# The output projection in native float32 instead of three float32r passes

## Chip, core and metric

The kernel runs on one core of one Trainium2 chip. The metric is the device time of one execution in microseconds (us).

## What is computed

One block of a streaming encoder on x of shape (1, 2048, 1024) in float32: normed rows go through one input projection (1024 to 2560); of its five parts of 512 columns three feed stick-breaking attention with 8 heads and two a gated position mixing. Both results are normed, joined, and projected back:

```python
a_out = rmsnorm(a_out, out_norm_g[layer, :SB_WIDTH])
b_out = rmsnorm(b_out, out_norm_g[layer, SB_WIDTH:])
mix = jnp.concatenate([a_out, b_out], axis=-1)
x = x + jnp.einsum('bse,ed->bsd', mix, w_out[layer])          # the output projection
h = rmsnorm(x, norm_mlp_g[layer])
act = jnp.square(jax.nn.relu(jnp.einsum('bsd,df->bsf', h, w_up[layer])))
x = x + jnp.einsum('bsf,fd->bsd', act, w_down[layer])
return rmsnorm(x, norm_final_g)
```

The output projection multiplies 2048 x 1024 by 1024 x 1024.

## The kernel before

**Tiling.** The 2048 rows go in four chunks of 512 (TC), each of four row blocks of 128. Matmul operands are kept as two float32r halves, hi and lo, made by `split` (lines 78 to 85): ScalarE writes hi (line 81, or line 84 where a column of factors is multiplied in), VectorE writes lo = source - hi (line 82, or 85). `mm3` (lines 87 to 90) then issues three matmuls for a product: hi x hi, hi x lo, lo x hi, all into one PSUM tile.

**Order.** Each engine runs its instructions in the order in which the program issues them. `together` advances one generator (`main`) step by step and, after each step, the attention generator (`side`) by a ratio, 0.8 in the output projection of chunks 0 and 1 (R_O). So projection, attention and MLP are interleaved on TensorE in an order that is fixed in the program. Chunks 0 and 1 run their last part beside attention; after attention has ended, chunks 2 and 3 run together: operands of chunk 3, its projection, operands of chunk 2, its projection, with the end of chunk 1's MLP and the turning of rows between them.

**Output projection.** `out_operands` (lines 421 to 457) loads the gated rows (`b_d`, tile `o_st`), squares them for the norm, transposes them on TensorE (line 438) and splits them from PSUM into `bm` (line 440); it loads the attention rows (`a_d`), which already lie the other way around, and splits them into `am` (line 455). Both live in tiles named `hT` (for chunk 3 `hTx`, on the other side of SBUF). POOL adds up the squares of the attention rows in `a_sq` (line 454). `out_weights` loads four slices of 128 x 512 of w_out and splits them with the factor `outg` (line 460, through `weight` and lines 84 and 85); SyncE's queue issues the loads. `out` (lines 463 to 489) runs four groups, two column halves times two operands; a group has four row blocks, and each row block takes four products (e = 0 to 3) of a 128 x 128 piece of `hT` with a 128 x 512 piece of `w`, twelve matmuls, into one of three PSUM tiles `mm` (one of five for chunk 3). VectorE adds the result to `y` with the row factor (line 478). Line 484 sums the squares over partitions by native float32 matmuls of one column.

Native float32 matmuls stand in two more places: line 239 (position mixing, 128 columns) and line 153 (128 columns). Lines 334, 438 and 501 are transposes.

`turn` (from line 491) norms the new rows and transposes them for the MLP; `up` and `down` use `mm3` too and aren't touched.

Of the kernel before, what the change touches and what calls it, by code (L numbers as in the profile page):

```python
# [16 lines left out]
P = 128  # L17
# [17 lines left out]
def block_kernel(ctx: ExitStack, tc: tile.TileContext, x, x_t, gmix, w_in, ln_g, ln_b, sgw, sgb,  # L35
# [4 lines left out]

    # ---- constants
    ident = const.tile([P, P], F32, name="ident")
# [19 lines left out]

    # ---- what one phase leaves for another
    q_d = dram.tile([NH, 2, HD, T], F32, name="q_d")
# [5 lines left out]
    def rsqrt_mean(pool, ssq, n, count, tag):  # L70
        """(ssq / count + EPS) ** -0.5 over [P, n]"""
        m = pool.tile([P, NTB], F32, name=f"{tag}_m", bufs=2)
        nc.vector.tensor_scalar(m[:, :n], ssq, 1.0 / count, EPS, ALU.mult, ALU.add)
        r = pool.tile([P, NTB], F32, name=f"{tag}_r", bufs=2)
        nc.gpsimd.tensor_tensor(r[:, :n], m[:, :n], mhalf[:, :n], ALU.pow)
        return r

    def split(hi, lo, src, scale=None):
        """hi + lo = src (times scale), hi and lo of 12 bits each"""
        if scale is None:  # L80
            nc.scalar.activation(hi, src, AF.Copy)  # L81
            nc.vector.tensor_tensor(lo, src, hi.bitcast(F32), ALU.subtract)  # L82
        else:
            nc.scalar.activation(hi, src, AF.Copy, scale=scale)
            nc.vector.scalar_tensor_tensor(lo, src, scale, hi.bitcast(F32), ALU.mult, ALU.subtract)
# [5 lines left out]

    # ---------------------------------------------------------------- projection
    class Rows:
        """where the normalized rows of one chunk live during the projection"""

# [12 lines left out]
    def proj(cs, places, sp, gated_first):  # L108
        """q, k, v and the gated rows of the chunks cs; the rows' 1 / rms joins after the products"""
        rs, r_rows = [], []  # L110
# [38 lines left out]
        def spread(pl, r4):  # L149
            """the chunk's r along the free axis, on all partitions"""  # L150
            ps = pl.ps()
            for tb in range(NTB):
                nc.tensor.matmul(ps[:, tb * P:(tb + 1) * P], r4[tb].broadcast_to([P, P]), ident,
                                 start=True, stop=True)
            rr = sp.tile([P, TC], F32, name="r_row", bufs=2)
            nc.scalar.activation(rr, ps, AF.Copy)
            r_rows.append(rr)
# [37 lines left out]
        def evac_v(pl, t0, i, ps):  # L195
            st = sp.tile([P, NH, 2, HD], F32R, name="qkv_st", bufs=2)
            split(st[:, :, 0, :], st[:, :, 1, :], ps.rearrange("p (h d) -> p h d", d=HD), rs[i])
            # the last ones don't hold up the loads behind them
            queue = nc.scalar if cs[-1] == NC - 1 else nc.sync
            queue.dma_start(v_d[t0 // TC, :, :, t0 % TC // P].rearrange("h p x d -> p h x d"), st.bitcast(F32))  # L200

        def gelu(dst, ps, r):
            """x * sigmoid(2 sqrt(2/pi) (x + a x^3)), the tanh form, of x = r ps"""
            t = sp.tile([P, 512], F32, name="gelu_t", bufs=3)
            nc.scalar.activation(dst, ps, AF.Copy, scale=r)
            nc.scalar.activation(t, dst, AF.Square)
            nc.vector.tensor_scalar(t, t, GELU_A, 1.0, ALU.mult, ALU.add)
            nc.vector.tensor_tensor(t, t, dst, ALU.mult)
            nc.scalar.activation(t, t, AF.Sigmoid, scale=GELU_B)
            nc.vector.tensor_tensor(dst, dst, t, ALU.mult)  # L210
# [61 lines left out]

    # ---------------------------------------------------------------- attention
    NKK = 3
# [5 lines left out]
    def attention(cs):  # L280
        """a step: weights of one block of queries, transposes of an earlier one, product with v of one before"""
        units = [(c, h, seg) for c in cs for h in range(NH) for seg in range(c, -1, -1)]
        state = {}

        def weigh(u, tb):
# [20 lines left out]
            ql = qt[:, tb * P:(tb + 1) * P]  # L306
            # fewer than 256 columns would take longer
            Z = max(L, 2 * P)
# [66 lines left out]

    # ---------------------------------------------------------------- output projection, MLP
    FG, RL_BUFS, ST_BUFS, W_BUFS = 2, 2, 4, 9
    NG = DFF // (P * FG)

    class Place:  # L380
        """where the rows of one chunk live"""

# [5 lines left out]

        def hT(self):
            return self.pool.tile([P, 2, 4, TC], F32R, name=f"hT{self.tag}", bufs=2)  # L390

# [6 lines left out]
    class Block:  # L398
        """the last part of the chunks cs, weights loaded once for all of them"""

# [4 lines left out]
        def normed_rows(self, src, dst, gain, tag):  # L405
            """dst = RMS norm of the rows of src [P, D], with the gain"""
            mp = self.mp
            junk = mp.tile([P, D], BF16, name="rl", bufs=RL_BUFS)
            ssq = mp.tile([P, 1], F32, name=f"{tag}_ssq", bufs=2)
            nc.scalar.activation(junk, src, AF.Square, accum_out=ssq)  # L410
            r = rsqrt_mean(mp, ssq, 1, D, tag)
            nc.vector.scalar_tensor_tensor(dst, src, r[:, 0:1], gain, ALU.mult, ALU.mult)
# [8 lines left out]
        def out_operands(self, i, weights_too=False):  # L421
            mp, c, pl = self.mp, self.cs[i], self.places[i]
            # b part
            bm, rbs = pl.hT(), []
            for tb in range(NTB):
# [13 lines left out]
                ts_ = slice(tb * P, (tb + 1) * P)  # L439
                split(bm[:, 0, :, ts_], bm[:, 1, :, ts_], ps)  # L440
            yield
            ws = self.out_weights(0, 1) if weights_too else None
            # a part
            am = pl.hT()
            total = mp.tile([P, TC], F32, name="a_sq", bufs=1)
            for e in range(4):
                st = mp.tile([P, TC], F32, name="o_st", bufs=4)
                nc.sync.dma_start(st, a_d[e * P:(e + 1) * P, c * TC:(c + 1) * TC])
                if e == 0:
                    nc.scalar.activation(total, st, AF.Square)  # L450
                else:
                    sq = mp.tile([P, TC], F32, name="rl", bufs=RL_BUFS)
                    nc.scalar.activation(sq, st, AF.Square)
                    nc.gpsimd.tensor_tensor(total, total, sq, ALU.add)
                split(am[:, 0, e, :], am[:, 1, e, :], st)
            self.mix[i] = bm, rbs, ws, am, total
            yield

        def out_weights(self, half, part):
            return [self.weight([512], w_out[k * P:(k + 1) * P, half * 512:(half + 1) * 512], outg_t[:, k:k + 1])  # L460
                    for k in range(part * 4, part * 4 + 4)]

        def out(self, i):
            """the rows of x plus the output projection"""
            c, pl = self.cs[i], self.places[i]
# [5 lines left out]
            def group(half, part, m, ws, rr):  # L471
                hs = slice(half * 512, (half + 1) * 512)
                for tb in range(NTB):
                    ts_ = slice(tb * P, (tb + 1) * P)
                    ps = pl.ps()
                    for e in range(4):
                        mm3(ps, m[:, 0, e, ts_], m[:, 1, e, ts_], ws[e][:, 0, :], ws[e][:, 1, :], e == 0, e == 3)
                    nc.vector.scalar_tensor_tensor(ys[tb][:, hs], ps, rr[tb], ys[tb][:, hs], ALU.mult, ALU.add)
                    yield
# [11 lines left out]
        def turn(self, i):  # L491
            """normed rows, split, the other way around"""
            pl = self.places[i]
# [13 lines left out]
        def up(self, fg):  # L507
# [3 lines left out]
            wus = []  # L511
            # the first group goes by half chunks, whose rows are ready earlier
            parts = 2 if fg == 0 else 1
# [29 lines left out]
        def down(self, fg, acts, finish=False):  # L543
            """finish: both halves of a row block at once, so that its rows are done early"""
            def half_weights(half):
# [42 lines left out]
        def middle(self):  # L588
            """all but the last product; returns that one"""
            acts = yield from self.up(0)  # L590
# [8 lines left out]
    def together(main, side=None, ratio=0.0):  # L599
        """side advances by ratio steps per step of main, up to the end of main, whose return value is returned,  # L600
        or of side (then OPEN is)"""
        due = 0.0
# [13 lines left out]
    ps_mm = ctx.enter_context(tc.tile_pool(name="ps_mm", bufs=3, space=PSUM))  # L616
    # what is free first at the end of the projection lies lowest, where the next pool's first tiles come
    ln_g_t = sp.tile([P, 512], F32, name="ln_g_t")
# [106 lines left out]
```

## Time and profile before

| | us |
|---|---|
| median of the two runs | 2592.94 |
| lowest and highest | 2591.4, 2594.48 |
| profiled execution, span from first to last instruction | 2591.2 |
| TensorE busy in it | 2521.4 |
| VectorE busy | 1795.8 |
| ScalarE busy | 1223.2 |
| POOL busy | 164.4 |

For the profiled execution the profile states its span alone; the two runs lie 0.2 and 3.3 us above it. Durations below come from that execution. PE is TensorE, PEld its weight loads, DVE VectorE, ACT ScalarE, SP SyncE, and L90 is line 90 of the kernel. Matmuls are pipelined and their ends are modelled, so that what one costs in a row of them is read from the distance of their starts, and not from its duration.

### The profile page before, as it was taken

What the parts mean: (1) busy time and instruction counts of PE and PEld (TensorE: products, weight loads), DVE (VectorE), ACT (ScalarE), POOL (GpSimd) and SP (SyncE); (2) the same over time, 40 slices, a digit from 0 to 9 for tenths busy, and PEclk for the clock granted to TensorE, in tenths of its full rate; (3) what the DMA queues carried; (4) which work ended last, traced back from release to release, by engine and by line L of the source; (5) the groups of instructions that cost most, each with busy time, mean ns of one, the idle gap of its engine ahead of it and who ended that gap; (6) DMA issues with size and microseconds to landing.
All of it is one profiled execution on the core that took longest, in us unless ns stands there. A gap on an engine that the chain in (4) does not pass through costs nothing.

```text
span 2591.2 us, 33154 instructions
## 1 busy us (share of the span) xinstructions
PE 2521.4 (97%) x11904; PEld 2047.3 (79%) x11904; DVE 1795.8 (69%) x2722; ACT 1223.2 (47%) x2306; POOL 164.4 (6%) x175
## 2 busy tenths in 40 slices
PE   7999998999999999999999999999999999999998
PEld 5788776777878888777788888877888888888886
DVE  6634688778888888899888888875833434344445
ACT  6314456455556555565655555663533232222222
POOL 3200022010000000011000000011100000000000
PEclk9999999999999999999999999999999999999999
DMA  6246756556443444346343334343311111111111
GB/s 211 97 127 207 217 158 193 155 175 192 130 123 118 122 123 122 122 123 196 98 121 116 117 117 122 108 145 98 131 54 47 46 49 49 49 49 45 45 45 66
DMA packets 160229, 299.99 MB, mean 116 GB/s; under 512 B 16576, under 2 KB 32960, under 8 KB 160064
## 3 DMA queue, kind: packets, MB, share of 16 engines
q1 hardware_dynamic: 155760, 295.77, 37.1%
q10 hardware_dynamic: 4304, 2.10, 0.3%
q8 instruction: 94, 1.54, 0.3%
q14 instruction: 71, 0.58, 0.1%
HBM read 255.86 MB, written 41.94 MB: 115 GB/s over the span
## 4 chain that ended last, share of the span: by engine, by line
PE 70%; DVE 20%; DMA 3%; issue 3%; ACT 3%; POOL 1%; SPq 0%; DVEq 0%; POOLq 0%; ACTq 0%
PE mm L89 20%; PE mm L90 20%; PE mm L88 20%; DVE pr L323 4%; DVE y L557 3%; PE tr L334 3%; DVE aT L82 2%; DVE b L324 2%; PE av L352 2%; PE av L353 2%; PE z L309 1%; PE z L310 1%; DVE pr L320 1%; DMA st<-in_w_in 1%; DVE w L82 1%
## 5 line engine op out<-in xcount | busy, mean ns | idle before, releaser
L81 ACT ACTIVATE w<-w_st 128x512 fp32r<-128x512 f32 x384 | 242.7, 634 | 457.1 <-PE mm L90 442.9
L82 DVE TENSOR_TENSOR w<-w_st,w 128x512 fp32r<-128x512 f32 x384 | 259.9, 685 | 163.8 <-ACT w L81 163.7
L90 PE MATMUL mm<-hT,w 128*128 128x512 f32 (+1 forms) x816 | 309.7, 379 | 0.0
L89 PE MATMUL mm<-hT,w 128*128 128x512 f32 (+1 forms) x816 | 308.7, 378 | 0.0
L88 PE MATMUL mm<-hT,w 128*128 128x512 f32 (+1 forms) x816 | 308.6, 378 | 0.1
L88 PE MATMUL mm<-w,act 128*128 128x512 f32 x768 | 300.8, 392 | 2.1 <-DVE y L557 1.4
L90 PE MATMUL mm<-w,act 128*128 128x512 f32 x768 | 301.6, 393 | 0.0
L89 PE MATMUL mm<-w,act 128*128 128x512 f32 x768 | 300.6, 391 | 0.0
L557 DVE TENSOR_TENSOR y<-mm,y 128x512 f32<-128x512 f32 x384 | 257.7, 684 | 49.9 <-PE mm L90 49.3
L323 DVE TENSOR_TENSOR_SCAN pr<-kk,pr,zeros 128x513 f32<-128x513 f32 x192 | 245.4, 1279 | 33.8 <-ACT kk L315 33.7
L315 ACT ACTIVATE kk<-z 128x512 f32<-128x512 f32 (+2 forms) x320 | 168.7, 527 | 176.4 <-PE z L310 122.3
L535 ACT ACTIVATE rl<-mm 128x512 f32<-128x512 f32 x128 | 76.5, 597 | 327.1 <-PE mm L90 326.9
L82 DVE TENSOR_TENSOR aT<-tr,aT 128x512 fp32r<-128x512 f32 (+1 forms) x320 | 190.7, 596 | 6.9 <-ACT aT L81 6.9
L334 PE MATMUL tr<-ident,b 128*128 128x128 f32 x1088 | 180.2, 275 | 6.1 <-DVE b L324 2.6
L81 ACT ACTIVATE aT<-tr 128x512 fp32r<-128x512 f32 (+1 forms) x320 | 172.7, 540 | 21.0 <-PE tr L334 20.4
L88 PEld LDWEIGHTS mm<-hT,w 128*128 128x128 f32 x816 | 154.0, 189 | 30.3 <-DVE y L557 0.5
L82 DVE TENSOR_TENSOR act<-rl,act 128x512 fp32r<-128x512 f32 x96 | 65.8, 686 | 161.0 <-ACT act L81 159.9
L90 PEld LDWEIGHTS mm<-hT,w 128*128 128x128 f32 x816 | 153.5, 188 | 29.4
L89 PEld LDWEIGHTS mm<-hT,w 128*128 128x128 f32 x816 | 153.5, 188 | 29.2
L88 PEld LDWEIGHTS mm<-w,act 128*128 128x128 f32 x768 | 144.6, 188 | 36.2 <-DVE y L557 3.7
L317 ACT ACTIVATE b<-z 128x512 f32<-128x512 f32 (+2 forms) x320 | 169.9, 531 | 0.0
L90 PEld LDWEIGHTS mm<-w,act 128*128 128x128 f32 x768 | 144.1, 188 | 31.3
(185 smaller groups left out, 5272.0 us busy)
## 6 DMA issues: line engine op xcount, KB each, us to landing
w_st<-in_w_up SPq DMA_DIRECT2D x192, 256.0 KB, 2.8
w_st<-in_w_down SPq DMA_DIRECT2D x192, 256.0 KB, 2.8
kt<-k_d SPq DMA_DIRECT2D x160, 256.0 KB, 4.7
st<-in_w_in SPq DMA_DIRECT2D x60, 512.0 KB, 5.2
vt<-v_d SPq DMA_DIRECT2D x80, 256.0 KB, 3.0
w_st<-in_w_out SPq DMA_DIRECT2D x64, 256.0 KB, 3.4
st<-in_x_t SPq DMA_DIRECT2D x16, 512.0 KB, 4.8
st<-in_x SPq DMA_DIRECT2D x16, 512.0 KB, 4.8
```

What stands on the lines that cost most here:

```text
L81: nc.scalar.activation(hi, src, AF.Copy)
L82: nc.vector.tensor_tensor(lo, src, hi.bitcast(F32), ALU.subtract)
L88: nc.tensor.matmul(ps, lh, rh, start=first, stop=False)
L89: nc.tensor.matmul(ps, lh, rl, start=False, stop=False)
L90: nc.tensor.matmul(ps, ll, rh, start=False, stop=last)
L315: nc.scalar.activation(kk[:, :L], z[:, :L], AF.Sigmoid, scale=-QK_SCALE)
L317: nc.scalar.activation(b[:, :L], z[:, :L], AF.Sigmoid, scale=QK_SCALE)
L323: nc.vector.tensor_tensor_scan(pr[:, ::-1], kk[:, ::-1], zeros, carry[tb], ALU.mult, ALU.add)
L324: nc.vector.tensor_tensor(b, b, pr[:, 1:TC + 1], ALU.mult)
L334: nc.tensor.transpose(tr[:, tb * P:(tb + 1) * P], bs[tb][:, j * P:(j + 1) * P], ident)
L535: nc.scalar.activation(rl, ps, AF.Relu)
L557: nc.vector.tensor_tensor(y[:, hs], ps, y[:, hs], ALU.add)
```

## The change

The operands of the output projection are no longer split. `hT` tiles for `bm` and `am` become float32, and VectorE copies the transposed rows and the attention rows into their first half; ScalarE writes the scaled weights as float32 into the first half of `w`, and the low half isn't made. Each product is one matmul on float32 operands where it was three on float32r operands. Sizes and numbers of the tiles stay, and so do all DMAs; the MLP, the attention and the input projection are as before. (The diff also drops comments, which are left out here.)

```diff
-        def hT(self):
-            return self.pool.tile([P, 2, 4, TC], F32R, name=f"hT{self.tag}", bufs=2)
+        def hT(self, dtype=F32R):
+            return self.pool.tile([P, 2, 4, TC], dtype, name=f"hT{self.tag}", bufs=2)
...
-            bm, rbs = pl.hT(), []
+            bm, rbs = pl.hT(F32), []
...
-                split(bm[:, 0, :, ts_], bm[:, 1, :, ts_], ps)
+                nc.vector.tensor_copy(bm[:, 0, :, ts_], ps)
...
-            am = pl.hT()
+            am = pl.hT(F32)
...
-                split(am[:, 0, e, :], am[:, 1, e, :], st)
+                nc.vector.tensor_copy(am[:, 0, e, :], st)
...
         def out_weights(self, half, part):
-            return [self.weight([512], w_out[k * P:(k + 1) * P, half * 512:(half + 1) * 512], outg_t[:, k:k + 1])
-                    for k in range(part * 4, part * 4 + 4)]
+            ws = []
+            for k in range(part * 4, part * 4 + 4):
+                st = self.mp.tile([P, 512], F32, name="w_st", bufs=ST_BUFS)
+                nc.sync.dma_start(st, w_out[k * P:(k + 1) * P, half * 512:(half + 1) * 512])
+                w = self.mp.tile([P, 2, 512], F32, name="w", bufs=W_BUFS)
+                nc.scalar.activation(w[:, 0], st, AF.Copy, scale=outg_t[:, k:k + 1])
+                ws.append(w)
+            return ws
...
                     for e in range(4):
-                        mm3(ps, m[:, 0, e, ts_], m[:, 1, e, ts_], ws[e][:, 0, :], ws[e][:, 1, :], e == 0, e == 3)
+                        nc.tensor.matmul(ps, m[:, 0, e, ts_], ws[e][:, 0, :], start=e == 0, stop=e == 3)
```

## Rows read from the trace of the kernel before

**Rows 1.** The page, parts 1 and 2: busy time; granted clock in tenths.

```profile
PE 2521.4 (97%) x11904; PEld 2047.3 (79%) x11904; DVE 1795.8 (69%) x2722; ACT 1223.2 (47%) x2306; POOL 164.4 (6%) x175
...
PEclk9999999999999999999999999999999999999999
```

**Rows 2.** The page, part 4: the chain that ended last, by line.

```profile
PE mm L89 20%; PE mm L90 20%; PE mm L88 20%; DVE pr L323 4%; DVE y L557 3%; PE tr L334 3%; DVE aT L82 2%; DVE b L324 2%; PE av L352 2%; PE av L353 2%; PE z L309 1%; PE z L310 1%; DVE pr L320 1%; DMA st<-in_w_in 1%; DVE w L82 1%
```

**Rows 3.** Stretches: from:to, length, busy PE, PEld, DVE, ACT, POOL; clock, DMA.

```profile
584.00:638.00 54.00, 52.39 (x258) 42.37 (x256) 46.21 (x73) 28.62 (x54) 3.56 (x6) 1.00 0.67 213
1178.00:1246.00 68.00, 64.80 (x316) 52.26 (x314) 63.38 (x96) 37.22 (x73) 4.95 (x7) 1.00 0.55 168
1755.70:1801.40 45.70, 45.70 (x201) 36.89 (x200) 22.56 (x33) 11.00 (x17) 1.46 (x1) 1.00 0.24 81
1817.00:1868.30 51.30, 49.94 (x239) 40.76 (x238) 40.53 (x68) 24.90 (x46) 7.67 (x10) 1.00 0.46 154
```

**Rows 4.** Groups by line and form, PE: count | busy us, mean ns | idle before.

```profile
L89 PE MATMUL mm<-w,hT 128*128 128x512 f32 x192 | 75.9, 396 | 0.0
...
L89 PE MATMUL mm<-w,hTx 128*128 128x512 f32 x64 | 25.5, 399 | 0.0
```

**Rows 5.** Timeline of PE in chunk 2's projection: start us, us, instruction.

```profile
1842.33 0.39 PE L88 MATMUL mm<-w,hT 128*128 128x512 f32 x1
...
1853.21 0.39 PE L88 MATMUL mm<-w,hT 128*128 128x512 f32 x1
```

**Rows 6.** Timeline of PE in chunk 3's projection.

```profile
1758.51 0.39 PE L88 MATMUL mm<-w,hTx 128*128 128x512 f32 x1
...
1764.11 0.39 PE L88 MATMUL mm<-w,hTx 128*128 128x512 f32 x1
```

**Rows 7.** Lines 239 and 484, native float32: durations ns min/median/max, first and last start.

```profile
L239 PE MATMUL mm<-vn,sgw_t x96: 270/275/275, 81.1 to 475.9; 128*128 128x128 f32 x96
...
L484 PE MATMUL mm<-ones,a_sq x32: 164/250/250, 591.4 to 1834.1; 128*128 128x1 f32 x32
```

**Rows 8.** The chain in order of time, two native pieces: start us, us, what.

```profile
81.23 1.78 PE mm L239 x16
...
591.55 0.79 PE mm L484 x8
```

**Rows 9.** Float32r of 256 columns: its group, then PE's timeline in chunk 2's first up.

```profile
L89 PE MATMUL mm<-hT,w 128*128 128x256 f32 x96 | 27.1, 283 | 0.0
...
1878.08 0.28 PE L88 MATMUL mm<-hT,w 128*128 128x256 f32 x1
...
1879.88 0.28 PE L88 MATMUL mm<-hT,w 128*128 128x256 f32 x1
```

**Rows 10.** Groups by line and form, DVE and ACT.

```profile
L85 DVE SCALAR_TENSOR_TENSOR w<-w_st,outg_t,w 128x512 fp32r<-128x512 f32 x64 | 47.3, 762 | 8.6 <-ACT w L84 8.3
...
L207 DVE TENSOR_SCALAR gelu_t<-gelu_t 128x512 f32<-128x512 f32 x32 | 19.9, 623 | 18.4 <-ACT gelu_t L206 18.1
...
L82 DVE TENSOR_TENSOR hT<-o_st,hT 128x512 fp32r<-128x512 f32 x12 | 12.7, 1075 | 1.9 <-ACT hT L81 1.8
...
L84 ACT ACTIVATE w<-w_st,outg_t 128x512 fp32r<-128x512 f32 x64 | 44.6, 723 | 51.5 <-PE mm L90 32.4 <-DMA w_st<-in_w_out 18.8
```

**Rows 11.** PE's waits (us, times, longest) in 564:587, 1145:1187 and 1801:1822.

```profile
PE mm L88 <- ACT w L84: 1.0, 1, 1.0
PE mm L88 <- DVE hT L82: 1.0, 1, 1.0
...
PE av L353 <- DVE aT L82: 2.3, 5, 0.9
...
PE mm L88 <- DVE y L557: 0.8, 1, 0.8
PE mm L438 <- DVE hT L82: 0.8, 1, 0.8
```

**Rows 12.** A stretch after chunk 0's operands, columns as in group 3.

```profile
578.10:581.50 3.40, 3.40 (x8) 2.50 (x9) 3.40 (x4) 3.40 (x7) 1.72 (x2) 0.54 0.92 281
```

## Prediction

> **What bounds the kernel now.** I read the page's parts on busy time and clock first. TensorE is busy for 2521.4 of 2591.2 us and its granted clock stands at the full 2.4 GHz level in all forty slices to within a tenth [rows 1]. The chain that ended last, by line, runs 20% each through L88, L89 and L90, the three lines of mm3 [rows 2]. So a change in the number or price of matmuls goes nearly straight into the time, unless the stretch in which it lies has idle TensorE time. That I read from the busy time by stretch, with one stretch for each of the four runs of the output projection (chunk 0, chunk 1, chunk 3, chunk 2, in this order of time): TensorE is busy for 52.4 of 54, 64.8 of 68, 45.7 of 45.7 and 49.9 of 51.3 us [rows 3]. VectorE is second (93% busy in chunk 1's stretch), but TensorE is the bound in all four. The whole projection is therefore a sum of matmul prices, corrected by a few us of idle time.
>
> **What the change removes and adds on TensorE.** There are 4 chunks, 4 groups each, 4 row blocks and 4 slices: 256 products of 128x128 by 128x512. The groups by line and form show them as 192 records on each of three lines for the chunks in hT and 64 on each for chunk 3 in hTx [rows 4]: 768 matmuls go.
>
> The duration of one (396 and 399 ns) includes the way through the array and is no price; the price is the distance of starts. In hT, 48 records lie between the starts at 1842.33 and 1853.21: 10.88 / 48 = 227 ns each, 680 ns a product [rows 5]. In hTx, 24 records lie between 1758.51 and 1764.11: 233 ns each, 700 ns a product [rows 6].
>
> What a native float32 product of 512 columns costs no row shows. The nearest rows are native products of other sizes. L239 multiplies in float32 already, with 128 columns: 64 products in the code, but 128 records (96 in vn here, 32 in vnx), and L484 (one column) has 32 records for 16 products [rows 7]. So one native instruction is two records, each with its own weight load, where a float32r one is one record. The changed projection is then 512 records where it was 768.
>
> Now the price of a record. Sixteen native records of 128 columns advance the chain by 1.78 us, 111 ns each; eight of one column advance it by 0.79 us, 99 ns each [rows 8]. Nearly the same for 128 times the columns: at this size the weight load sets the distance, and 111 ns is only an upper bound for streaming 128 columns. Taken up to 512 columns it bounds a record at 4 x 111.3 = 445, say 448 ns, a product at 896 ns. From below, a record can't be cheaper than a float32r one of the same size, since both stream 512 four-byte columns: 227 ns, a product at 453 ns.
>
> Between them I go by durations. Float32r records of 256 columns last 283 ns and start 120 ns apart (15 between 1878.08 and 1879.88) [rows 9]; with 512 columns they start 227 ns apart. So a column streams in (227 - 120) / 256 = 0.417 ns, one cycle at 2.4 GHz, and 13 ns are fixed. The shortest native record of one column lasts 164 ns and the shortest of 128 columns 270 ns [rows 7]: 106 ns for 127 columns, 0.83 ns a column, two cycles. A native record of 128 columns lasts about as long as a float32r record of 256. I take two cycles: 427 ns for 512 columns. The fixed part can't be more than 111.3 - 106.7 = 4.6 ns, or 128 columns would be further apart than they are. One record is then 431 ns and one product 863 ns; in hTx, where a float32r record costs 6.6 ns more, 876 ns.
>
> A rule of the Trainium skill speaks against the change in the same direction. FP8 and Floating Point Precision, section TensorE Precision Notes, says that true FP32 takes four passes through the array, where the split takes three. If each pass cost what a float32r matmul costs here, fixed part included, the sum would be larger than mine; it has its own place among the rivals.
>
> The sum on TensorE: (863 - 680) x 192 = +35.1 us, (876 - 700) x 64 = +11.3 us, together **+46.4 us**. With no fixed part (854 ns everywhere): 33.4 + 9.9 = +43 us. With 448 ns a record, and the surcharge in hTx: 41.5 + 13.4 = +55 us.
>
> **What it takes from the other engines.** VectorE loses the 64 low halves of the output weights at L85, 47.3 us, and ScalarE the high halves of the operands. In out_operands 32 subtractions at L82 become 32 copies; those from o_st are long today (1075 ns mean) [rows 10]. The trace has no float32 copy on VectorE; a single-source operation of 128x512 in SBUF takes 623 ns at L207, so I put a copy there, with the 1075 ns of today's operation as the upper bound and nothing as the lower, none of it on the path. ScalarE keeps the 64 scaled copies at L84, 723 ns each. No DMA comes or goes: the 64 loads of w_out stay on SP's queue in the same place.
>
> All this lies beside TensorE, so it pays only where TensorE waits today. Around the four operand stages these waits are: chunk 0, 1.0 us for the weights from ScalarE and 1.0 us for hT from VectorE; chunk 1, five waits of 2.3 us for aT, while VectorE is behind with operands and weights; chunk 2, 0.8 us for hT and 0.8 us for y [rows 11]. Together 5.9 us. Part stays: the copy of hT still stands in VectorE's queue behind attention's scans. I take 4 us. The most that could go is these and all idle time of the four stretches, 5.9 + (1.6 + 3.2 + 0 + 1.4 from the four stretches [rows 3]) = 12 us; the least is nothing. No wait is added: a product waits for one writer per operand where it waited for two. If the copies were late, transposes at L438 would wait for their PSUM buffer as today.
>
> The clock: right after these two waits of TensorE in chunk 0 the granted clock is 0.54 for 3.4 us, nearly the 1.2 GHz level [rows 12]. Half of 3.4 us, 1.7 us, is what this costs now; it may come back if the wait shrinks, or stay. It lies inside the 4 us and its bounds.
>
> **Sum.** The span is 2591.2 us and the two runs lie 0.2 and 3.3 us above it, their median 1.7; I add to the median. 2592.9 + 46.4 - 4 = **2635 us**, 1.6% slower. The forecast's own range: 43 - 12 = +31 gives 2624; 55 - 0 gives 2648.
>
> **Rivals.**
> 1. *Four passes at the full price.* A record pays the fixed 13 ns in each of two passes: 4 x 227 = 907 ns in hT, 933 in hTx; 43.6 + 14.9 - 4 = +54.5, 2647 us. For it: float32r shows that fixed part at 256 and 512 columns. Against it: at 128 columns a record would take 2 x (53 + 13) = 133 ns, and takes 111.
> 2. *A record streams one column a cycle*, as float32r does; this one ends on the other side. The product then costs 453 ns (467 in hTx): -43.5 - 14.9 - 4 = -62, 2531 us. For it: native records of one and of 128 columns are nearly equally far apart, so no distance here shows the second cycle. Against it: the 106 ns between their shortest durations. It decides as soon as a product costs less than some 680 ns.
> 3. *The relief reaches further than the waits.* VectorE, 93% busy in chunk 1's stretch, sheds some 50 us. If besides the 12 us another 5 to 10 us of late attention tiles beside these stretches vanish, the time is about 2592.9 + 46.4 - 20 = 2619 us. Against it: TensorE has only 6.2 us of idle time in the 219 us of the stretches, and it runs in program order, so that freed VectorE time doesn't let it start more.
>
> **Chances and range.** Forecast 0.73, rival 1 0.09, rival 2 0.07, rival 3 0.10, else 0.01. About 2% (52 us, so above 2645 or below 2541) is what a measurement can tell here from no change. The forecast's middle, rival 3 and the lower part of rival 1 lie within it; most of rival 1 and the upper edge of the forecast lie above it: 0.12 slower, 0.07 faster (rival 2), 0.81 within. The range goes from rival 3 to a little over rival 1, 2618 to 2650 us, and leaves out rival 2 and the edges.
>
> **What would show it.** Distances of starts in the matmuls on w and hT: 431 ns between records, two a product (rival 1: 454, rival 2: 227). The stretch of chunk 3, which is nothing but products, goes from 45.7 to about 57 us (rival 1: 60.6, rival 2: 30.8). The part after 1890 us and the attention between keep their lengths. The waits for w at L84 and hT shrink, the five for aT in chunk 1 too. Wrong would be: a granted clock at the lower level through these products, new idle time before them, or a record that isn't twice the float32r one.

## The result and the profile after

The changed kernel takes 2633.77 us (two runs, 2633.75 and 2633.79) against 2592.94: the ratio is 1.0158, with a 95% interval of 1.0128 to 1.0187. Timed again later, beside more runs of the kernel before, it gave 2629.0 us, ratio 1.0143 (1.0130 to 1.0157). So it is 37 to 41 us slower, within 2%. The forecast was 2635 us.

The page of the changed kernel: busy time (part 1), the granted clock in 40 slices (part 2), the chain that ended last by line (part 4).

```profile
PE 2559.8 (97%) x11648; PEld 2002.1 (76%) x11648; DVE 1752.1 (67%) x2658; ACT 1206.2 (46%) x2274; POOL 160.7 (6%) x175
...
PEclk9999998999999999999999999999999999999999
...
PE mm L90 18%; PE mm L89 18%; PE mm L88 18%; PE mm L483 5%; DVE pr L323 3%; PE tr L334 3%; DVE y L563 3%; PE av L352 2%; PE av L353 2%; DVE b L324 2%; DVE aT L82 2%; PE z L309 1%; PE z L310 1%; DVE pr L320 1%; DVE w L82 1%
```

Against [rows 1] TensorE has 256 records less and 38.4 us more of busy time; VectorE has 43.7 us less. The native products, now L483, are 5% of the chain that ended last, and VectorE's 64 low halves of [rows 10] are gone. The four projection stretches, in the columns of [rows 3]:

```profile
575.80:641.90 66.10, 66.10 (x202) 33.77 (x203) 43.72 (x67) 31.85 (x62) 8.72 (x10) 1.00 0.68 218
1186.30:1257.20 70.90, 70.90 (x228) 37.88 (x227) 51.77 (x74) 33.45 (x66) 5.99 (x7) 1.00 0.48 149
1772.80:1828.60 55.80, 55.80 (x137) 25.16 (x136) 14.75 (x21) 11.24 (x17) 1.02 (x1) 1.00 0.21 69
1845.60:1907.00 61.40, 59.80 (x169) 28.34 (x168) 31.93 (x52) 23.70 (x44) 5.34 (x9) 1.00 0.37 120
```

TensorE has no idle time left in the first three, and VectorE's share in chunk 1 has fallen from 93% to 73%.

**The price.** Line 483 by duration, and the chain in order of time at the start of chunk 3's projection (start us, us, what):

```profile
L483 PE MATMUL mm<-w,hT x384: 590/592/697, 575.8 to 1906.6; 128*128 128x512 f32 x192
...
L483 PE MATMUL mm<-w,hTx x128: 592/592/676, 1772.8 to 1828.2; 128*128 128x512 f32 x128
```

```profile
1772.96 13.73 PE mm L483 x32
```

There are 384 + 128 = 512 records, two a product, and 13.73 / 32 = 429 ns each. Over all neighbouring records of L483 the median distance of starts is 429 ns in hT and 429 ns in hTx. A product costs 858 ns, where three float32r records cost 680 in hT and 700 in hTx [rows 5, 6]. The price of the change on TensorE is (858 - 680) x 192 + (858 - 700) x 64 = 34.2 + 10.1 = **44.3 us**.

**Where the rest went.** I cut the spans at TensorE's own marks: the first product of a projection, the first and the last transpose of the turn after it, and the first transpose of the operands (in us, worked out from the starts in the timelines; the last two kernels are experiments that are told below). Each column is one execution. Up to the first transpose of chunk 0's operands nothing that the change touches has run, and this transpose starts at 570.9 us before and at 571.3, 569.2, 568.7 and 569.3 in the others, in the table's order; so the first row also holds up to 2.2 us of difference between executions.

| stretch | before | changed | again | copies on ScalarE | split kept |
|---|---|---|---|---|---|
| operands 0, from 564 us | 12.3 | 11.8 | 10.0 | 9.2 | 10.8 |
| projection 0 | 58.8 | 66.1 | 66.1 | 66.1 | 67.9 |
| turn 0 | 16.2 | 14.0 | 14.0 | 14.0 | 14.0 |
| middle of chunk 0 | 505.1 | 505.0 | 504.9 | 504.7 | 505.0 |
| operands 1 | 22.9 | 25.4 | 25.0 | 23.6 | 24.5 |
| projection 1 | 63.2 | 70.9 | 71.0 | 70.9 | 72.3 |
| turn 1 | 16.8 | 14.3 | 14.2 | 14.3 | 14.3 |
| middle of chunk 1 | 466.3 | 466.3 | 466.0 | 466.4 | 466.5 |
| operands 3, end of chunk 1's MLP | 30.1 | 35.0 | 33.1 | 29.0 | 30.7 |
| projection 3 | 45.7 | 55.8 | 55.8 | 55.8 | 55.8 |
| operands 2 | 16.5 | 17.0 | 16.9 | 16.0 | 16.6 |
| projection 2, turn 3 | 50.2 | 61.4 | 61.4 | 62.1 | 60.8 |
| turn 2 | 9.4 | 11.3 | 12.7 | 12.8 | 12.8 |
| rest | 713.6 | 713.7 | 713.7 | 713.7 | 713.7 |

The projections grow by 7.3, 7.7, 10.1 and 11.2 us, together 36.3, which is 8 us less than the price; the 8 us lie in projections 0 to 2. Chunk 3's, which was already full of products, grows by the price to the digit (64 x 0.158 = 10.1). The turns of chunks 0 and 1 shrink by 4.7 us; chunk 2's grows by 1.9, since TensorE waits 1.9 us for the last y there, where it waited 0.6 before. And the operand stretches, where I expected relief, grow: +2.5 for chunk 1, +4.9 for chunk 3, +0.5 for chunk 2, -0.5 for chunk 0.

Projections 0, 1 and 2 before, cut at the table's marks (columns of [rows 3]); after, they are the first, second and fourth row of the fence with the projection stretches:

```profile
576.30:635.00 58.70, 57.50 (x265) 45.99 (x266) 51.79 (x76) 32.60 (x63) 8.60 (x8) 0.97 0.74 239
1179.30:1242.50 63.20, 61.83 (x295) 49.79 (x294) 59.48 (x89) 32.42 (x64) 4.40 (x6) 1.00 0.58 176
1818.00:1868.10 50.10, 48.74 (x233) 40.01 (x233) 39.33 (x64) 23.89 (x43) 7.62 (x10) 1.00 0.46 153
```

Of the 8 us, 2.3 are idle time (1.2, 1.4 and 1.4 us before; 0, 0 and 1.6 after), and some 1.7 are the lowered clock of [rows 12], which lies in the first of these rows. The other 4 us no run isolates. They lie in time that the profile counts as busy; as a float32r record lasts 396 ns and the next starts 227 ns after it, short waits between records would be counted there too.

The 4.9 us is easy to see. TensorE's wait in that stretch, then VectorE's timeline (start us, us, instruction, idle time before it and what ended it):

```profile
PE mm L88 <- DVE y L563: 3.0, 1, 3.0
```

```profile
1742.20 1.23 DVE L455 COPY hTx<-o_st 128x512 f32<-128x512 f32 x3
1745.57 0.62 DVE L455 COPY hTx<-o_st 128x512 f32<-128x512 f32 x1 [2.13 <-DMA o_st<-a_d]
1746.11 1.87 DVE L563 TENSOR_TENSOR y<-mm,y 128x512 f32<-128x512 f32 x3
```

The copy of the fourth slice of attention rows stands at the head of VectorE's queue and waits 2.13 us for its DMA. Three additions to y stand behind it, the PSUM tiles that they would free are missing to TensorE, and TensorE waits 3.0 us. In the kernel before the same place reads:

```profile
1730.75 0.69 DVE L82 TENSOR_TENSOR hTx<-o_st,hTx 128x512 fp32r<-128x512 f32 x1 [0.73 <-ACT hTx L81]
1731.36 0.68 DVE L557 TENSOR_TENSOR y<-mm,y 128x512 f32<-128x512 f32 x1
1731.96 1.19 DVE L82 TENSOR_TENSOR hTx<-o_st,hTx 128x512 fp32r<-128x512 f32 x1
```

There the high half on ScalarE came between DMA and VectorE, and the additions to y lie between the four subtractions. That isn't the order of the program, where the four stand in one loop (lines 446 to 455) with no addition to y between them: the build lays out each engine's queue anew, and in the changed kernel the four copies come first. That they come first because ScalarE's step is gone is my reading; no run shows it. (My description of the kernel before took the order for that of the program; the queues of the two kernels differ around the projection on TensorE too.)

The wait costs more than itself, as the stretches right after the two long waits show (columns of [rows 3]):

```profile
1746.80:1752.60 5.80, 5.75 (x14) 4.50 (x15) 2.50 (x4) 1.35 (x2) 0.88 (x1) 0.50 0.85 305
1171.90:1175.50 3.60, 3.58 (x9) 2.82 (x10) 3.60 (x7) 1.58 (x5) 0.63 (x1) 0.57 0.84 290
```

After TensorE had been idle for 3.0 us the granted clock is 0.50 for 5.8 us, the 1.2 GHz level, although TensorE is busy throughout. Half of 5.8 us, 2.9 us, goes there. Wait and clock make 5.9 us, less the 0.5 us of waiting for y that stood in this stretch before; it grew by 4.9. In chunk 1 it is the same: VectorE waits 2.0 us for three of the copies' DMAs, TensorE 3.4 us for aT behind them, then 3.6 us at 0.57:

```profile
DVE hT L455 <- DMA o_st<-a_d: 2.0, 3, 1.3
PE av L353 <- DVE aT L82: 3.4, 1, 3.4
```

### The profile page after: what moved, and what is told of

It reads as the page before. It is cut to its first block, busy times and chain, and to the rows that moved or that the text cites. A ratio compares the mean times of both kernels' runs of the same rounds, so it can differ in the third digit from the quotient of the medians.

```text
span 2632.0 us, 32502 instructions
## 1 busy us (share of the span) xinstructions
PE 2559.8 (97%) x11648; PEld 2002.1 (76%) x11648; DVE 1752.1 (67%) x2658; ACT 1206.2 (46%) x2274; POOL 160.7 (6%) x175
## 4 chain that ended last, share of the span: by engine, by line
PE 71%; DVE 17%; issue 4%; ACT 3%; DMA 3%; POOL 2%; SPq 0%; DVEq 0%; POOLq 0%; ACTq 0%
PE mm L90 18%; PE mm L89 18%; PE mm L88 18%; PE mm L483 5%; DVE pr L323 3%; PE tr L334 3%; DVE y L563 3%; PE av L352 2%; PE av L353 2%; DVE b L324 2%; DVE aT L82 2%; PE z L309 1%; PE z L310 1%; DVE pr L320 1%; DVE w L82 1%
## 5 line engine op out<-in xcount | busy, mean ns | idle before, releaser
L88 PEld LDWEIGHTS mm<-w,act 128*128 128x128 f32 x768 | 145.2, 189 | 40.0 <-DVE y L563 6.7
L483 PE MATMUL mm<-w,hT 128*128 128x512 f32 x384 | 169.7, 593 | 0.6 <-ACT w L465 0.6
```

What stands on the lines that cost most here:

```text
L88: nc.tensor.matmul(ps, lh, rh, start=first, stop=False)
L483: nc.tensor.matmul(ps, m[:, 0, e, ts_], ws[e][:, 0, :], start=e == 0, stop=e == 3)
```

## The experiments

Each ratio is to runs of the kernel before beside it, whose medians were 2593.48, 2592.14 and 2592.47 us.

| kernel | median us | ratio to before (95%) |
|---|---|---|
| changed, again | 2629.00 | 1.0143 (1.0130 to 1.0157) |
| three passes, no split | 2591.40 | 0.9992 (0.9983 to 1.0001) |
| three passes, no split, copies on ScalarE | 2583.55 | 0.9967 (0.9956 to 0.9979) |
| native, split kept | 2629.61 | 1.0141 (1.0128 to 1.0155) |
| native, copies on ScalarE | 2625.93 | 1.0127 (1.0111 to 1.0142) |
| native, half columns | 2631.21 | 1.0146 (1.0132 to 1.0159) |
| three passes, lows on POOL | 2603.74 | 1.0049 (1.0036 to 1.0062) |
| three passes, split once | 2600.83 | 1.0030 (1.0018 to 1.0042) |

**Is it the price? Three passes without the split.** Edit to the changed kernel (with the tiles in float32r):

```diff
-                        nc.tensor.matmul(ps, m[:, 0, e, ts_], ws[e][:, 0, :], start=e == 0, stop=e == 3)
+                        mm3(ps, m[:, 0, e, ts_], m[:, 0, e, ts_], ws[e][:, 0, :], ws[e][:, 0, :], e == 0, e == 3)
```

> The operands are prepared as in the changed kernel (one copy each, no low half), but written as float32r, and each product is three float32r matmuls of the high halves. Left out: the low halves, so that the result is three times the product of the rounded operands; the three matmuls of a product cost TensorE what they cost before. Theory (the loss is the price of the native records, and what the other engines are spared is worth a few us): 2586 to 2592 us, the four projection stretches no longer than before, but DVE's direct copies from o_st wait for their DMA in the operand stretches of chunks 1 and 3 as in the changed kernel (3 us of TensorE waits each). Rival (the order in which the instructions were laid out anew, not the price, makes much of the 41 us): 2600 us or more.

It is as fast as the kernel before, to within 0.2%. Nearly all else of the change is in it, the queues laid out anew included, so the loss is the native products. The theory missed chunk 1: its operands take 22.9 us, as before, and TensorE's wait for aT there is 0.8 us, where the changed kernel has 3.4. Inside, two effects nearly cancel: projections 0, 1 and 2 and the turns after 0 and 1 are 1.4, 2.0, 0.4, 1.3 and 1.2 us shorter than before, while operands 3 takes 35.5 us, as in the changed kernel, with the same wait:

```profile
PE mm L88 <- DVE y L563: 3.5, 1, 3.5
...
1719.70:1755.20 35.50, 32.01 (x137) 26.18 (x136) 16.45 (x29) 14.98 (x29) 6.67 (x8) 0.90 0.61 203
```

**Are the copies the wait? Copies on ScalarE, with both kinds of products.**

```diff
-                nc.vector.tensor_copy(am[:, 0, e, :], st)
+                nc.scalar.activation(am[:, 0, e, :], st, AF.Copy)
```

> The changed kernel with the 16 copies of attention rows from o_st into hT (line 455) on ScalarE instead of VectorE. Theory (these copies hold up VectorE's queue while they wait for the DMA, y is not added up behind them, TensorE waits 3.0 and 3.4 us and then runs at half clock for some us): both waits go, chunk 3's operand stretch falls from 35.0 to about 30, chunk 1's from 25.4 to about 21.5; total 2623 to 2627 us. Rival (the waits are due to something else in that stretch, and come back in another place): 2632 to 2636 us.

> Three float32r matmuls of the high halves without the low halves (the low halves are left out of the result), as run before, but with the copies of attention rows on ScalarE. Theory (the copies at the head of VectorE's queue cost chunk 3's operand stretch 5 us and chunk 2's 1 us there, as they do in the changed kernel, and nothing else is wrong with these stretches): 2583 to 2587 us, the operand stretch of chunk 3 at 29 to 30 us. Rival: 2590 us or more, with the waits in another place.

In both, the stretch of operands 3 is full: TensorE is busy for 29.0 of 29.0 us at the full clock. First with native products, then with three passes:

```profile
1733.10:1762.10 29.00, 29.00 (x137) 24.28 (x136) 14.54 (x25) 16.55 (x33) 6.63 (x8) 1.00 0.72 249
```

```profile
1719.70:1748.70 29.00, 29.00 (x137) 24.28 (x136) 14.95 (x25) 16.43 (x33) 6.65 (x8) 1.00 0.71 247
```

The theory holds for chunk 3: 6 and 6.5 us. With three passes the whole falls from ratio 0.9992 to 0.9967, and the intervals are apart. With native products it falls to 1.0127, whose interval overlaps that of the changed kernel. For chunk 1 the theory was too good: operands 1 come down to 23.6 us only, where 21.5 was expected, with three smaller waits in place of the long one:

```profile
PE av L352 <- ACT aT L81: 1.3, 1, 1.3
PE av L353 <- DVE aT L82: 0.8, 1, 0.8
PE tr L334 <- DVE b L321: 0.5, 1, 0.5
```

Now ScalarE holds the copies, and the aT that TensorE waits for longest is written by ScalarE after them. Norms of finished rows stand between the two, so that the copies aren't shown to be its only cause.

**What is the relief? Native products with all of the splitting work.** ScalarE and VectorE do what they did before; the low halves are made and not read:

```diff
-                nc.vector.tensor_copy(bm[:, 0, :, ts_], ps)
+                split(bm[:, 0, :, ts_], bm[:, 1, :, ts_], ps)
...
-                nc.vector.tensor_copy(am[:, 0, e, :], st)
+                split(am[:, 0, e, :], am[:, 1, e, :], st)
...
-                nc.scalar.activation(w[:, 0], st, AF.Copy, scale=outg_t[:, k:k + 1])
+                split(w[:, 0], w[:, 1], st, outg_t[:, k:k + 1])
```

> Native products as in the changed kernel, but ScalarE and VectorE do all the work of splitting as before (the low halves are made and not read). Theory A (the few us of relief come from the work that VectorE and ScalarE no longer do): 2593 + 44 = 2637 us or more, with the waits of before back in the stretches. Theory B (longer products cover the old waits by themselves, and the direct copies cost more than they spare, because they wait for their DMA at the head of VectorE's queue): 2626 to 2631 us, with chunk 3's operand stretch back at about 30 us (35 in the changed kernel) and chunk 1's back at 22 to 23 us (25.4).

2629.61 us, theory B; A's 2637 or more lies outside the interval, which ends at 1.0155 x 2593.5 = 2633.7 us. Sparing VectorE some 44 us of busy time is worth nothing in sum, as long as VectorE makes the direct copies: projections 0 and 1 are 1.7 and 1.4 us longer than in the changed kernel, operands 3 4.3 us shorter (30.7, as B said; operands 1, at 24.5, came down by 0.9 only). The turns of chunks 0 and 1 are as short as in the changed kernel, so with native products that gain doesn't need the spared work. Turn 0 before, after, and with three passes without the split, in the columns of [rows 3]:

```profile
635.00:651.50 16.50, 12.51 (x72) 9.68 (x71) 14.09 (x23) 14.22 (x30) 1.86 (x2) 0.90 0.17 48
```

```profile
641.90:656.00 14.10, 10.73 (x71) 7.93 (x70) 13.54 (x21) 12.09 (x26) 1.32 (x1) 1.00 0.26 76
```

```profile
633.60:648.50 14.90, 10.77 (x70) 8.14 (x69) 13.64 (x23) 13.75 (x30) 1.86 (x2) 1.00 0.20 54
```

Idle time is 4.0 us before and 3.4 after; the clock is 0.90 before and 1.00 after. A mean of 0.90 over 16.5 us is 3.3 us at the lower level, which costs 1.65 us; with the 0.6 us of idle time that makes most of the 2.4. The clock's part isn't earned by the native products alone: in the third row it isn't lowered either, at 4.1 us of idle time. In the turn of chunk 1 TensorE's wait for y is 2.6 us before, in three passes without the split, and in the same with the copies on ScalarE; the mean clock is 0.90, 1.00 and 0.90. Over the turns of chunks 0 and 1 the clock was lowered in five of ten with three passes (five executions), and in none of ten with native products, where that wait is 1.4 to 1.5 us. In chunk 2's turn it was lowered in four of the five native executions, which is why that row reads 12.7 and 12.8 us beside 11.3. So some 1.7 us in each turn come and go with the execution.

**Fixed part or column price? Half columns.**

```diff
+                    for q in range(2):
+                        qs = slice(q * 256, (q + 1) * 256)
...
+                            nc.tensor.matmul(ps[:, qs], m[:, 0, e, ts_], ws[e][:, 0, qs], start=e == 0, stop=e == 3)
```

> The changed kernel with each native product of 512 columns made as two of 256 columns: 1024 records where the changed kernel has 512. Theory (two cycles a column and a fixed 2 ns a record): starts 216 ns apart, the whole +1 to +2 us on the changed kernel, 2634 to 2637 us. Rival (a native record of this size carries the fixed 13 ns of a float32r record, hidden at 512 columns): starts 227 ns or more apart, 2646 us.

The chain at chunk 3's projection, and the durations of the records:

```profile
1768.72 13.81 PE mm L485 x64
```

```profile
L485 PE MATMUL mm<-w,hT x768: 377/379/483, 575.1 to 1903.9; 128*128 128x256 f32 x192
```

13.81 / 64 = 216 ns a record. A native record is 0.833 ns a column, two cycles at 2.4 GHz, and 2.3 ns: 213.3 + 2.3 at 256 columns, 426.7 + 2.3 at 512. The total, 2631 us, is below the 2634 to 2637 us expected, which were counted from 2633.8; it lies between the two timings of the changed kernel. The durations agree: 592 - 379 = 213 ns for 256 columns.

**Are the differences the chip's? The changed kernel again.**

> The changed kernel once more, beside more runs of the kernel before, to place it against the variants: 2631 to 2635 us. If the direct copies on VectorE are what costs it, it stays 6 to 9 us above its variant with the copies on ScalarE (2625.9) and 2 to 5 us above native products with the full splitting work (2629.6); if these differences were those of the chip, they vanish here.

In the total, mostly yes. 2629.0 us is below the 2631 to 2635 us expected, 3 us above the variant with copies on ScalarE, not 6 to 9, and level with the one that keeps the split; in total these three are not apart. What the table by stretch shows is steadier: operands 1 25.0 and operands 3 33.1 us, both longer than with the copies on ScalarE. The wait behind the copies is 2.2 us here where it was 3.0, because the last slice's DMA made VectorE wait 0.90 us instead of 2.13. So this piece of the loss varies from execution to execution, and 1.8 us of the difference between the two profiles lies before the projection begins. The kernel with half columns, which has the same copies, shows it once more: a wait of 2.2 us too, but a clock that wasn't lowered after it (1.00 over the stretch, 0.95 here), and 31.6 us (columns of [rows 3]):

```profile
1737.00:1768.60 31.60, 29.35 (x138) 24.24 (x137) 15.63 (x29) 15.09 (x29) 6.81 (x8) 1.00 0.66 228
```

**Can three passes be had cheaper?** Three passes without the split and with the copies on ScalarE are 0.3% faster than before, but leave the low halves out. Two versions with full precision tried for that gain. First, POOL makes the low halves of the weights:

```diff
-            split(w[:, 0], w[:, 1], st, scale)
...
+                nc.scalar.activation(st, st, AF.Copy, scale=scale)
+                nc.scalar.activation(w[:, 0], st, AF.Copy)
+                nc.gpsimd.tensor_tensor(w[:, 1], st, w[:, 0].bitcast(F32), ALU.subtract)
```

> The kernel before (three float32r passes), with the low halves of the output weights made by POOL instead of VectorE: ScalarE scales the loaded slice in place and writes the high half, POOL subtracts. Theory (VectorE's work in the projection stretches is worth what three passes without splitting showed there and in the turns, some 6 us, and no copy waits for a DMA): 2585 to 2590 us. Rival (POOL, at 1.5 us for an operation of 128x512, and ScalarE's second pass make the weights late and TensorE waits for them): 2595 us or more.

The rival's time came; its wait came only in part. The group on POOL (count | busy us, mean ns | idle), and TensorE's waits for weights, all in chunk 0, and in the turn of chunk 3:

```profile
L423 POOL TENSOR_TENSOR w<-w_st,w 128x512 fp32r<-128x512 f32 x64 | 88.3, 1400 | 92.0 <-ACT w L422 80.6 <-PE tr L334 11.2
...
PE mm L88 <- ACT w L422: 2.9, 2, 2.5
...
PE mm L506 <- DVE n_m L73: 6.0, 1, 6.0
```

A slice takes 1400 ns on POOL, where VectorE takes 762 [rows 10]. Operands 1 grow to 26.5 us, and projection 2 with turn 3 to 57.8. No wait for weights stands there; TensorE waits 6.0 us for n_m, a step of the norm of new rows in the turn. Small steps of the norms run on POOL too (line 75), between the slices; that they held up the turn fits, but no run isolates it. Second, the weights are split once, kept in DRAM and loaded as halves by the later chunks:

```diff
...
+                if self.cs[0] == 0:
+                    w = self.weight([512], w_out[...], outg_t[:, k:k + 1])
+                    nc.sync.dma_start(wo_d[k, half], w.bitcast(F32))
+                else:
+                    w = self.mp.tile([P, 2, 512], F32R, name="w", bufs=W_BUFS)
+                    nc.sync.dma_start(w.bitcast(F32), wo_d[k, half])
...
```

> The kernel before (three float32r passes, full precision), but the output weights are split once, for chunk 0, written to DRAM as two halves, and loaded as such for the three other chunks: 48 operations of 0.75 us each leave VectorE and ScalarE, and 48 loads are 512 KB instead of 256 KB. Theory (the relief that three passes without splitting showed, 8.5 us with the copies on ScalarE, comes in good part from the weights): 2584 to 2590 us. Rival (the loads now go straight into the buffers that TensorE frees, wait for them at the head of SyncE's queue and hold up the MLP's loads behind them): 2595 us or more, with TensorE waiting for weights after the projection.

The loss is real, its place is neither theory's. Projection 1 gains 2.4 us (60.8), but chunk 0, which stores the halves, loses 5.9 us in its projection (64.7). (Its row of operands is 3.5 us longer too, but 3.3 of these lie before the first transpose of the operands, at 574.2 us, and the first store is issued at 581.6.) SyncE's queue during chunk 0 (waited for: us in total, times, longest):

```profile
SPq L465 <- DVE w L86: 26.2, 14, 9.5
```

The stores wait there for VectorE's low halves, 26.2 us in all, with every load behind them. That this is what the projection loses fits, but no run isolates it. Projection 2 loses 2.5 us more, whose cause I didn't follow. No version that beats the kernel before was found.

## Why the prediction was right, point by point

- **TensorE is the bound, so the price goes into the time**: right. Projection 3 grew by the price exactly; with three passes left and all else changed the time didn't move.
- **Two records a product**: right, 512 records. **Two cycles a column**: right; the durations of 1 and 128 columns, which carried this choice, gave 0.83 ns, and 256 to 512 columns give 0.832. Rival 2 falls.
- **The fixed part**: predicted at most 4.6 ns, measured 2.3. Rival 1 falls: four passes at float32r's price would be 907 ns, and it is 858. The Trainium skill's rule (FP8 and Floating Point Precision, TensorE Precision Notes: four passes for true FP32) agrees with the trace in time: 858 ns is four times 213.3 ns (512 columns at 2.4 GHz) and 5 ns. Three split passes are cheaper, but by 20%, not 25%, since each of them pays some 13 ns that a native pass doesn't.
- **The surcharge in hTx**: wrong term, 13 ns a product. Native records cost 429 ns in both places; 0.8 us of the sum. The sum on TensorE was 46.4 us, and is 44.3.
- **Relief of 4 us**: the size came out by luck (44.3 - 40.8 = 3.5 in the first profile, some 7 by the second timing); the mechanism was wrong. The term stood for waits of TensorE that vanish, and named those of [rows 11]. But in the operand stretches the change lost 7.4 us net, and over the whole span TensorE's idle time (span less busy time) rose from 69.8 to 72.2 us. The step that failed is "No wait is added: a product waits for one writer per operand". That holds for the products; but the copies themselves now wait for the DMA at the head of VectorE's queue, where ScalarE had waited before, and TensorE waits 3.0 and 3.4 us behind them. The prediction asked what the copy stands behind, and of late copies feared only for the transposes at L438; it didn't ask what else stands behind the copy: the additions to y and aT. Against that stand 8 us in projections 0 to 2, of which only 2.3 are idle time, and in the turns 4.7 less 1.9.
- **The clock** was put inside the 4 us. At the start of chunk 0's projection it is no longer lowered; after the new waits it is, for 5.8 and 3.6 us. With the two turns before, it costs some 5 us in either profile, so that it gave nothing in sum.
- **Rival 3**, that shedding VectorE work is worth more than the waits: falls. With native products and the work kept the total is the same. With three passes and the copies on ScalarE it is worth 8.6 us (2592.14 - 2583.55), still less than the 12 us of the forecast's own bound.
- **Signs named in advance**: 431 ns a record (429), chunk 3's stretch at 57 us (55.8), the part behind the projection unchanged (713.6, 713.7), the waits for w at L84 smaller (1.0 to 0.6 us). Two spoke against the prediction: the five waits for aT in chunk 1 didn't shrink, 2.3 us in all became one of 3.4; and new idle time came ahead of chunk 3's products, 3.0 us where 0.5 had stood.

## What to carry to other kernels

Where TensorE is the bound, count a change of matmul precision by the distance of starts, and take native float32 at 858 ns for 128x128 by 128x512 against 227 ns for each float32r pass, both at the full clock: three passes beat it as long as the split hides on other engines. Removing a step between a DMA and an in-order engine moved the wait for the DMA to that engine here: look at what stands behind it in the queue, and give the first touch of loaded data to the engine that has the least behind it. A wait of 3 us on TensorE cost nearly twice that here, since the clock was lowered after it; after a wait of 2.2 us it was lowered in one execution and not in another. So place stretches against each other over several executions, and with their granted clock, before a difference of 2 us is given a cause.

## What the runs showed that was not expected

A float32r record carries a fixed 13 ns (227 ns at 512 columns, 120 at 256) and 6 to 7 ns more in chunk 3, whose operands lie in hTx; a native record carries 2.3 ns in either place (429 and 216). Both stream behind a weight load of the same shape (about 190 ns long each), so why float32r pays more is open. VectorE's float32 copy of 128x512 takes 428 ns from SBUF in the median of the 12 into hT (415 to 1426), less than the 623 ns that I had taken from another operation, and 680 ns from PSUM.
